# Sums of squares from token-major copies of x, modulation weights loaded ahead of x, and part of block 1's h made earlier

## The chip, the core and the metric

The kernel runs on one core of a Trainium2 chip. The core has a matrix engine (TensorE, PE in the profile), a vector engine (VectorE, DVE), a scalar engine (ScalarE, ACT), a general engine (GpSimd, POOL) and a queue that only issues transfers (SyncE, SP). Each takes its own instructions in order and waits on semaphores for the others; sixteen DMA engines move the data. The metric is the device time of one execution in microseconds (us), the median of the runs.

## The reference, cut to what matters

The layer takes 2048 tokens of 1024 features and 256 context tokens. For this document only its head matters, and that all of `h` enters one wide projection.

```python
def _rmsnorm(x, g):
    xf = x.astype(jnp.float32)
    xf = xf * lax.rsqrt(jnp.mean(xf * xf, axis=-1, keepdims=True) + EPS)
    return (xf * g.astype(jnp.float32)).astype(x.dtype)
...
mod = jax.nn.silu(c) @ w_ada[i] + b_ada[i]
mod_c = jax.nn.silu(c_ctx) @ w_ada[i] + b_ada[i]
shift, scale, gate = mod[:, None, :D], mod[:, None, D:2 * D], mod[:, None, 2 * D:]
h_lat = _rmsnorm(x, norm_g[i]) * (1.0 + scale) + shift
h_ctx = _rmsnorm(ctx, norm_g[i]) * (1.0 + scale_c) + shift_c
...
na_q, na_k, na_v, na_g, r_q, r_k, r_v, r_g = _split_proj(h_lat @ w_in)
```

So each token needs the mean square of its 1024 features, and each feature a scale and a shift, before its row of `h` can meet `w_in`. Attention, retention and the output projection follow.

## The kernel before

**Layout.** Matrix products want the features on the partitions, so the host gives a transposed copy `xT` beside `x`: nine groups of 256 tokens (0 to 7 latent, 8 the context), each of eight chunks k of 128 features. A group is held in two halves u of four chunks, 512 KB each. Two groups make a block of 512 tokens: block 0 is groups 0 and 1, block 1 groups 2 and 3, and so on; block 4 is the context.

**Precision.** Every wide product is made of three: a value is split into a high part (rounded to the fast matrix type, `hhi`, `whi`) and the rest (`hlo`, `wlo`), and high·high, high·low and low·high are added in PSUM. The high part is a copy on ACT, the low part a subtraction on DVE or POOL.

**What a group goes through.** `squares` (L194) squares it on ACT and adds the chunks on POOL (half 0) and DVE (half 1) until one 128 x 256 sum is left; `colsum` (L205) sums over partitions with four small matrix products; `rstd` (L212) takes the power -0.5 on DVE and POOL; `spread_copy` and `spread` (L218, L222) bring the result onto all partitions through PE. `spread_mul` (L238, L241) multiplies x by it; `prep_ab` (L267) applies scale and shift, some chunks on DVE (L272), the rest on ACT (L274); `prep_hl` (L276) makes the high part on ACT (L279) and the low part on DVE or POOL (L283, chosen by `LOV`), and notes a spill of the half to DRAM (`hS`, L253) at least eight steps later. The two groups of block 0 go chunk by chunk through `prep_first` (L255; L262 to L265) instead.

**Modulation.** Scale and shift come in four sets u of 256 features: four pieces of `w_ada` each (512 KB, `ada_load`), products on PE (`ada_mm`, L311, full fp32, or for the pieces named in `SPL` in split form after `ada_split`), a row copied out (`ada_row`, L319), turned by PE and finished on DVE (`ada_fin`, L324 to L332). Chunk k needs set k // 2.

**The windows.** `window(b)` (L491) is the first projection stage: for block b four units `u_k` (L380) of eight chunks k, three products (L363) per chunk, 32 steps per window; step n of window b is step 32b + n. Window 0 takes its units in the order `STEPS`, the others one unit after another. After a unit, ACT and DVE (L383, L384) split the result into a tile of `op` (two buffers) and SP stores it to `kS` (L151). The weight of units 0 and 1 is prepared in `w_split` (`wr[0]`), that of units 2 and 3 from `wr[1]`.

**The order.** `PLAN` (L39) lists every preparatory action with the step before whose successor it is put into the program (-1: before step 0); `run_acts` issues them. Names: sq squares, cs colsum, rs rstd and spread_copy, sp spread, mu spread_mul, ab and hl as above, s/m/ar/af the modulation, p prep_first, ws the weight split, x a load, blk a new block of h. Since each engine works in order, an action's place in the list is its place in every engine's queue. A step number is only a place in the program: an engine that is not waiting runs ahead of PE. SP carries the loads in `LOADS` order, then x loads, spills and kS stores as the program reaches them, and stops at the first whose data or buffer is not ready.

**Buffers.** Tiles named `st` (four buffers of 512 KB) take the raw weights, the squares of groups 2 to 7 and the context. Block 2 is written over the tiles in which x of groups 0 to 3 lay, so their spills must have landed first.

Of the kernel before, what the change touches and what calls it, by code (L numbers as in the profile page):

```python
# [18 lines left out]
P = 128  # L19
# [39 lines left out]
]  # L59
SPL = [9, 0, 1, 0]  # L60
ALO = [0, 5, 9, 4]
PFL = [3, 0, 0, 1, 0, 3, 1, 3]
STEPS = [0, 1, 2, 0, 1, 3, 2, 3, 2, 0, 3, 1, 1, 3, 0, 3, 2, 3, 0, 0, 2, 1, 1, 1, 1, 2, 3, 2, 2, 0, 3, 0]
WSL = [3, 2]
LEAD = 32
LOADS = [
# [16 lines left out]
def hybrid_kernel(ctx: ExitStack, tc: tile.TileContext, a: dict, out: bass.AP):  # L83
# [24 lines left out]
    sil4 = cst.tile([P, KC, 4], F32R, name="sil4")  # L108
    mods = cst.tile([P, 4, 3, 2, 2], F32, name="mods")
# [83 lines left out]

    def squares(i):  # L194
        sqs[i] = []
        for u in range(2):
            sq = xsq[i][u] if i < 2 else env["st"].tile([P, KH, 256], F32, name="st")
            nc.scalar.activation(sq, raw[i][u], AF.Square)
            eng = (nc.gpsimd, nc.vector)[u]
            eng.tensor_tensor(sq[:, 0:2, :], sq[:, 0:2, :], sq[:, 2:4, :], ALU.add)  # L200
            eng.tensor_tensor(sq[:, 0, :], sq[:, 0, :], sq[:, 1, :], ALU.add)
            sqs[i].append(sq)
        nc.vector.tensor_tensor(sqs[i][0][:, 0, :], sqs[i][0][:, 0, :], sqs[i][1][:, 0, :], ALU.add)

    def colsum(*ii):  # L205
        pm = ptile(None if ii[0] < 4 else psm)
        for j, i in enumerate(ii):
            for t in range(2):
                nc.tensor.matmul(pm[:, 2 * j + t:2 * j + t + 1], sqs[i][0][:, 0, t * P:(t + 1) * P], one, start=True, stop=True)
            rms[i] = pm[:, 2 * j:2 * j + 2]  # L210

    def rstd(i):  # L212
        r = env["st"].tile([P, 2], F32, name="rs", bufs=4)
        nc.vector.tensor_scalar(r, rms[i], 1.0 / D, EPS, ALU.mult, ALU.add)
        nc.gpsimd.tensor_tensor(r, r, mhalf[:, 0:2], ALU.pow)
        rbs[i] = r

    def spread_copy(i):  # L218
        rbs[i, 1] = env["st"].tile([P, 2, P], F32, name="t0", bufs=2)
        nc.vector.tensor_copy(rbs[i, 1], rbs[i].unsqueeze(2).to_broadcast([P, 2, P]))  # L220
# [34 lines left out]
    def prep_first(k):  # L255
        if k == KC - 1:
            spill.extend((i, u, now[0] + 8) for i in range(2) for u in range(2))
        for i in range(2):
            hi, lo = sub_dst(i)
            A, B = ab(i, k)  # L260
            x = raw[i][k // KH][:, k % KH, :]
            nc.scalar.activation(hi[:, k, :], x, AF.Identity, bias=B, scale=A)  # L262
            nc.vector.tensor_scalar(x, x, A, B, ALU.mult, ALU.add)
            eng = nc.gpsimd if PFL[k] >> i & 1 else nc.vector
            eng.tensor_tensor(lo[:, k, :], x, f(hi[:, k, :]), ALU.subtract)  # L265
# [27 lines left out]
    def ada_split(u, j):  # L293
        whl[u, j] = []
        for k in range(2):
            w = wad[4 * u + j][:, k, :]
            t = op.tile([P, 2, 512], F32R, name="o")
            nc.scalar.copy(t[:, 0, :], w)
            eng = nc.gpsimd if ALO[u] >> j & 1 else nc.vector
            eng.tensor_tensor(t[:, 1, :], w, f(t)[:, 0, :], ALU.subtract)  # L300
            whl[u, j].append(t)

    def ada_mm(u, j):
        if u not in aps:
            aps[u] = ptile(psm)
        for k in range(2):
            ops = [(silc, wad[4 * u + j][:, k, :])]
# [8 lines left out]
    def ada_row(u):  # L316
        rows[u] = op.tile([P, 2, 512], F32, name="o")[:, 0, :]
        n = 4 if SPL[u] else 2
        (nc.scalar.copy, nc.vector.tensor_copy)[u % 2](rows[u][0:n, :], aps[u][0:n, :])  # L319
# [132 lines left out]
    nc.sync.dma_start(silc, a["c2"])  # L452
    nc.scalar.activation(silc, silc, AF.Silu)
    nc.scalar.copy(sil4[:, :, 0:2], silc)
# [10 lines left out]
    for name, *args in LOADS:  # L465
        lds[name](*args)
    acts = dict(sq=squares, cs=lambda *i: colsum(*i), rs=lambda i: (rstd(i), spread_copy(i)), sp=lambda *i: spread(*i),
                mu=lambda i, u: spread_mul(i, (u,)), ab=prep_ab, hl=prep_hl, blk=alloc_blk, x=load_x, w=lambda: wr.append(w_raw(2560)),
                w2=lambda: load_w(), s=ada_split, m=ada_mm, ar=ada_row, af=ada_fin, p=prep_first,
                ws=lambda g: w01.append(w_split(wr[g], lo=WSL[g])))  # L470
    w01 = []
# [1152 lines left out]
```

## Time and profile before

| what | value |
|---|---|
| median of three runs | 1363.7 us (1363.22 to 1367.48) |
| the profiled execution | 1366.09 us |
| its span in the profile | 1364.1 us |
| mean granted TensorE clock | 0.993 |
| bytes moved by DMA | 287.25 MB, mean 211 GB/s |

The page of the profile gives busy shares over the whole span and the costliest groups of instructions. For a change at the head of the kernel the other views say more: the timeline of one engine (start, length, engine, line, operation, tiles, and in brackets how long the engine stood idle before it and what ended that), and the windows view (for each stretch of time the busy time of PE, weight loads, DVE, ACT and POOL with their instruction counts, then the granted clock of TensorE, the share of time in which the DMA engines were busy, and what they moved in GB/s). Transfers are shown where SP issues them, not where they land.

### The profile page before, as it was taken

To read this page: it belongs to the slowest core of one execution; us is meant where nothing else is said; L and a number is where in the kernel's file an instruction comes from. 1 tells how busy PE (TensorE), PEld (TensorE's weight loads), DVE (VectorE), ACT (ScalarE), POOL (GpSimd) and SP (SyncE) were. 2 spreads that over 40 slices of the span, in tenths; PEclk is the share of its full clock that TensorE was granted. 3 is DMA by queue.
4 is the path that set the end of the run, shared out by engine and by line. 5 is a ranking of instruction groups with operands and counts; after the bars stand their busy time and mean duration, and the time that the engine had idled before them with its cause. 6 is when DMAs were issued, how large, how long until landed. Compare 5 with 4: busy or idle time off the path is not lost.

```text
span 1364.1 us, 23087 instructions
## 1 busy us (share of the span) xinstructions
PE 1313.1 (96%) x8236; PEld 1148.9 (84%) x8236; DVE 827.9 (61%) x1442; ACT 606.5 (44%) x1259; POOL 583.8 (43%) x571
## 2 busy tenths in 40 slices
PE   6999999999999999999999999999999899999997
PEld 2477899887997788998999889889998789888886
DVE  5686356675766754377767777776644633445345
ACT  5354343243533344555655466556642234333332
POOL 5452102554034664355535465555422254544432
PEclk9999999999999999999999999999999999999999
DMA  9386788464867657967587778676538988455533
GB/s 364 132 277 232 260 296 222 165 208 151 326 179 228 217 197 230 273 198 194 157 225 208 210 202 245 171 215 188 140 110 277 267 264 286 159 170 170 162 121 128
DMA packets 197685, 287.25 MB, mean 211 GB/s; under 512 B 17345, under 2 KB 126017, under 8 KB 196290
## 3 DMA queue, kind: packets, MB, share of 16 engines
q1 hardware_dynamic: 165154, 228.35, 56.4%
q10 hardware_dynamic: 32416, 57.42, 11.7%
q8 instruction: 66, 1.08, 0.3%
q14 instruction: 49, 0.40, 0.1%
HBM read 194.48 MB, written 91.23 MB: 209 GB/s over the span
## 4 chain that ended last, share of the span: by engine, by line
PE 70%; DMA 9%; DVE 8%; ACT 4%; POOL 3%; issue 3%; SPq 2%; ACTq 0%; POOLq 0%; DVEq 0%
PE mm L374 17%; PE mm L671 13%; PE mm L1465 11%; PE mm L363 7%; PE sS L1025 4%; PE tr L1052 3%; PE po L1073 3%; PE mm L1188 2%; PE tr L1054 2%; PE po L1075 2%; DMA vB<-o 1%; PE mm L1377 1%; PE mm L1376 1%; PE mm L1375 1%; PE mm L311 1%
## 5 line engine op out<-in xcount | busy, mean ns | idle before, releaser
L374 PE MATMUL mm<-whi,hlo 128*128 128x256 f32 x832 | 228.5, 282 | 0.2 <-DMA hlo<-cS 0.2
L374 PE MATMUL mm<-whi,hhi 128*128 128x256 f32 x768 | 224.2, 292 | 0.0
L374 PE MATMUL mm<-wlo,hhi 128*128 128x256 f32 x768 | 216.9, 282 | 0.0
L1056 ACT CAST pt<-tr 128x640 fp32r<-128x640 f32 (+1 forms) x128 | 95.6, 747 | 160.9 <-PE tr L1054 158.4
L1062 DVE TENSOR_TENSOR pt<-tr,pt 128x640 fp32r<-128x640 f32 (+1 forms) x128 | 113.9, 890 | 78.5 <-ACT pt L1056 77.2
L374 PEld LDWEIGHTS mm<-whi,hlo 128*128 128x128 f32 x832 | 156.3, 190 | 0.6 <-DMA hlo<-cS 0.5
L1045 POOL TENSOR_SCALAR sp<-sp,stt 128x640 f32<-128x640 f32 (+2 forms) x128 | 103.2, 808 | 106.5 <-DVE stt L1044 74.5
L374 PEld LDWEIGHTS mm<-whi,hhi 128*128 128x128 f32 x768 | 146.2, 190 | 0.0
L374 PEld LDWEIGHTS mm<-wlo,hhi 128*128 128x128 f32 x768 | 145.9, 190 | 0.1
L1034 DVE CUSTOM_DVE_ANT_0 sp<-sS,nb 128x640 f32<-128x640 f32 (+2 forms) x128 | 105.6, 825 | 33.6 <-PE sS L1025 27.2
L1039 ACT ACTIVATE sp<-sp,stt 128x640 f32<-128x640 f32 (+2 forms) x128 | 107.4, 839 | 19.9 <-DVE stt L1034 18.7
L625 POOL TENSOR_TENSOR whi<-st,whi 128x512 fp32r<-128x512 f32 x48 | 63.9, 1353 | 107.3 <-ACT whi L624 107.3
L363 PE MATMUL mm<-hhi,whi 128*128 128x512 f32 x256 | 107.8, 421 | 0.0
L363 PE MATMUL mm<-hlo,whi 128*128 128x512 f32 x256 | 101.6, 397 | 6.0 <-DVE hlo L265 2.1
L1025 PE MATMUL sS<-k,q 128*128 128x256 f32 (+3 forms) x512 | 99.0, 315 | 5.3 <-DVE stt L1034 5.0
L363 PE MATMUL mm<-hhi,wlo 128*128 128x512 f32 x256 | 101.9, 398 | 0.3 <-DVE wlo L347 0.3
L671 PE MATMUL mm<-hhi,whi 128*128 128x512 f32 x336 | 98.4, 395 | 3.7 <-POOL whi L625 3.2
L1474 DVE TENSOR_TENSOR xt<-mm,xt 128x512 f32<-128x512 f32 x64 | 43.8, 686 | 87.4 <-PE mm L1465 87.3
L1465 PE MATMUL mm<-wor,y 128*128 128x512 f32 x384 | 95.6, 398 | 1.1 <-DVE xt L1474 1.1
L1025 PEld LDWEIGHTS sS<-k,q 128*128 128x128 f32 x512 | 82.7, 188 | 12.2 <-DVE stt L1034 8.4
L1465 PE MATMUL mm<-won,y 128*128 128x512 f32 x336 | 89.9, 406 | 0.0
L625 POOL TENSOR_TENSOR wlo<-st,wlo 128x512 fp32r<-128x512 f32 x36 | 53.6, 1488 | 77.4 <-ACT wlo L624 77.4
(258 smaller groups left out, 3057.5 us busy)
## 6 DMA issues: line engine op xcount, KB each, us to landing
st<-in_w_in_dram SPq DMA_DIRECT2D x64, 512.0 KB
q<-qS SPq DMA_DIRECT2D x64, 256.0 KB
hlo<-hS SPq DMA_DIRECT2D x20, 512.0 KB
k<-kS SPq DMA_DIRECT2D x16, 576.0 KB
kS<-o SPq DMA_DIRECT2D x16, 512.0 KB
vB<-o SPq DMA_DIRECT2D x64, 128.0 KB
qS<-o ACTq DMA_DIRECT2D x16, 512.0 KB
woS<-g ACTq DMA_DIRECT2D x32, 256.0 KB
```

Of the source, the lines that this page charges most:

```text
L363: nc.tensor.matmul(pm[:, :n], ww[:, k, cs], h[:, k, :], start=(k == 0 and i == 0), stop=(k == KC - 1 and i == 2))
L374: nc.tensor.matmul(pm[:, t * WG:(t + 1) * WG], h[:, k, o:o + P], ww[:, k, :], start=(k == 0 and i == 0), stop=(k == KC - 1 and i == 2))
L625: nc.gpsimd.tensor_tensor(t[:, 1], r, f(t)[:, 0], ALU.subtract)
L671: nc.tensor.matmul(pm, ww[:, k, :], hh[:, k, :], start=(k == 0 and i == 0), stop=(k == KH - 1 and i == 2))
L1025: nc.tensor.matmul(o, hd["q"][i][:, hl, j * P:(j + 1) * P], k, start=(hl == 0), stop=(hl == 1))
L1034: nc.vector.tensor_tensor_reduce(T["sp"][:, :n], T["s"], nbz[big][:, o:o + n], -1.0, 3e38, ALU.add, ALU.min, T["st"][:, 0:1])
L1039: nc.scalar.activation(sp[:, :n], sp[:, :n], AF.Exp, bias=st[:, 0:1], scale=-1.0, accum_out=st[:, 1:2])
L1045: nc.gpsimd.tensor_scalar(sp[:, :n], sp[:, :n], st[:, 2:3], 0.0, ALU.mult, ALU.add)
L1056: nc.scalar.copy(pt[:, :ng_ + 2, 0, :], tr[:, :ng_ + 2, :])
L1062: nc.vector.tensor_tensor(pt[:, :n, 1, :], tr[:, :n, :], f(pt)[:, :n, 0, :], ALU.subtract)
L1465: nc.tensor.matmul(pm, yy[:, k, :], ww[:, k, sl], start=(k == 0 and i == 0), stop=(k == 3 and i == 2))
L1474: nc.vector.tensor_tensor(xts[t][:, sl], pm, xts[t][:, sl], ALU.add)
```

## The change

For groups 2 to 8 a second load (`load_xt_`) brings the same 256 tokens from `x` itself, tokens on partitions, as two tiles of 128 x 1024 in `st`; ACT squares each with an accumulator, which gives the 128 sums at once. The adds and `colsum` of these groups go; `rstd` works in place. Groups 0 and 1 keep the old form, with both halves added on DVE and the spread copy on ACT.

The four pieces of modulation set 0 are loaded first, three of them ahead of group 1's x, and the pieces in split form change: before pieces 0 and 3 of set 0 and piece 0 of set 2, after it pieces 0 and 2 of set 3 (`SPL`). The others of set 3 use `silz`, a copy of `silc` with two columns of zeros, so that all of a set fill four rows.

The low parts move: `prep_first` takes group 1 first, with group 1's low part on POOL and group 0's on DVE; both halves of both weights in `ws` are subtracted on POOL, and are entered half by half; the split pieces are subtracted on DVE. `STEPS` becomes regular. In the plan, `ab` and `hl` of half 0 of groups 2 and 3 come at steps 14 to 17 (before: 24 to 28), the Squares of groups 2 and 3 at 9 and 10; from step 48 on the plan is as before except for the column sums that go and the `xt` loads at 60 and 81.

```diff
-SPL = [9, 0, 1, 0]
-ALO = [0, 5, 9, 4]
-PFL = [3, 0, 0, 1, 0, 3, 1, 3]
-STEPS = [0, 1, 2, 0, 1, 3, 2, 3, 2, 0, 3, 1, 1, 3, 0, 3, 2, 3, 0, 0, 2, 1, 1, 1, 1, 2, 3, 2, 2, 0, 3, 0]
-WSL = [3, 2]
+SPL = [0, 0, 0, 5]
+STEPS = [0, 1, 0, 1, 2, 3, 2, 3, 0, 1, 2, 3, 0, 1, 2, 3, 0, 1, 2, 3, 0, 1, 2, 3, 0, 0, 1, 1, 2, 2, 3, 3]
 LOADS = [
+    ('a', 0, 0), ('a', 0, 1), ('a', 0, 2), ('x', 1), ('c',), ('a', 0, 3), ('x', 0), ('a', 1, 0), ('a', 1, 1), ('w', 0), ('a', 1, 2),
+    ('a', 1, 3), ('w', 1), ('a', 2, 0), ('a', 2, 1), ('x', 2), ('a', 2, 2), ('a', 2, 3), ('x', 3), ('a', 3, 0), ('a', 3, 1), ('a', 3, 2), ('a', 3, 3),
 ]
+    (-1, 'm', 0, 0), (-1, 'm', 0, 1), (-1, 'm', 0, 2), (-1, 'sq', 1), (-1, 'm', 0, 3), (-1, 'cs', 1), (-1, 'rs', 1),
+    (-1, 'ar', 0), (-1, 'sq', 0), (-1, 'm', 1, 0), (-1, 'm', 1, 1), (-1, 'af', 0), (-1, 'sp', 1), (-1, 'cs', 0),
+    (-1, 'rs', 0), (-1, 'mu', 1, 0), (-1, 'ws', 0, 0), (-1, 'sp', 0), (-1, 'mu', 0, 0), (-1, 'p', 0), (-1, 'p', 1),
+    (-1, 'm', 1, 2), (-1, 'm', 1, 3), (0, 'ws', 0, 1), (0, 'ar', 1), (0, 'ws', 1, 0), (0, 'mu', 1, 1), (1, 'af', 1),
+    (1, 'p', 2), (2, 'mu', 0, 1), (3, 'p', 3), (3, 'ws', 1, 1), (3, 'xt', 2), (3, 'xt', 3), (3, 'x', 4),
+    (7, 'm', 2, 0), (7, 'm', 2, 1), (7, 'm', 2, 2), (7, 'm', 2, 3), (7, 'ar', 2), (8, 'af', 2), (8, 's', 3, 0),
+    (8, 'x', 5), (9, 'p', 4), (9, 'sq', 2), (10, 'sq', 3), (11, 'rs', 2), (11, 'm', 3, 0), (11, 'm', 3, 1),
+    (11, 'p', 5), (12, 'rs', 3), (12, 's', 3, 2), (13, 'sp', 2, 3), (13, 'mu', 2, 0), (13, 'xt', 4), (14, 'mu', 3, 0),
+    (14, 'ab', 2, 0), (15, 'm', 3, 2), (15, 'm', 3, 3), (15, 'blk', 1), (15, 'ab', 3, 0), (16, 'hl', 2, 0),
+    (16, 'ar', 3), (17, 'af', 3), (17, 'hl', 3, 0), (18, 'p', 6), (19, 'p', 7), (20, 'mu', 2, 1), (20, 'mu', 3, 1),
+    (20, 'sq', 4), (21, 'ab', 2, 1), (22, 'ab', 3, 1), (22, 'xt', 5), (23, 'hl', 2, 1), (24, 'hl', 3, 1),
+    (24, 'rs', 4), (28, 'x', 6), (32, 'sp', 4), (33, 'mu', 4, 0), (35, 'mu', 4, 1), (36, 'sq', 5), (40, 'ab', 4, 0),
+    (42, 'rs', 5), (46, 'xt', 6), (48, 'ab', 4, 1), (50, 'sp', 5), (52, 'mu', 5, 0), (52, 'sq', 6), (53, 'x', 7),
...
+    def load_xt_(i):
+        sqs[i] = []
+        src = a["ctx"] if i == 8 else a["x"][i * 256:(i + 1) * 256, :]
+        for t in range(2):
+            xt = env["st"].tile([P, KH, 256], F32, name="st").rearrange("p k t -> p (k t)")
+            nc.sync.dma_start(xt, src[t * P:(t + 1) * P, :])
+            sqs[i].append(xt)
+
     def squares(i):
+        if i >= 2:
+            rms[i] = env["st"].tile([P, 2], F32, name="rs", bufs=4)
+            for t, xt in enumerate(sqs[i]):
+                nc.scalar.activation(xt, xt, AF.Square, accum_out=rms[i][:, t:t + 1])
+            return
...
-            eng = (nc.gpsimd, nc.vector)[u]
+            eng = nc.vector if u or i < 2 else nc.gpsimd
...
-        nc.vector.tensor_copy(rbs[i, 1], rbs[i].unsqueeze(2).to_broadcast([P, 2, P]))
+        copy = nc.scalar.copy if i < 2 else nc.vector.tensor_copy
+        copy(rbs[i, 1], rbs[i].unsqueeze(2).to_broadcast([P, 2, P]))
...
-        for i in range(2):
+        for i in (1, 0):
...
-            eng = nc.gpsimd if PFL[k] >> i & 1 else nc.vector
+            eng = nc.gpsimd if i else nc.vector
...
+    def ws_half(g, u):
+        if u == 0:
+            w, wps[g] = w_parts(wr[g])
+            w01.append(w)
+        wps[g][u]()
```

More of the change, by code (lines that the diff above doesn't have):

```diff
@@ L108, in hybrid_kernel @@
     sil4 = cst.tile([P, KC, 4], F32R, name="sil4")
+    silz = cst.tile([P, KC, 4], F32, name="silz")
     mods = cst.tile([P, 4, 3, 2, 2], F32, name="mods")
@@ L205, in colsum @@
     def colsum(*ii):
-        pm = ptile(None if ii[0] < 4 else psm)
+        pm = ptile()
         for j, i in enumerate(ii):
@@ L212, in rstd @@
     def rstd(i):
-        r = env["st"].tile([P, 2], F32, name="rs", bufs=4)
+        r = rms[i] if i >= 2 else env["st"].tile([P, 2], F32, name="rs", bufs=4)
         nc.vector.tensor_scalar(r, rms[i], 1.0 / D, EPS, ALU.mult, ALU.add)
@@ L298, in ada_split @@
             nc.scalar.copy(t[:, 0, :], w)
-            eng = nc.gpsimd if ALO[u] >> j & 1 else nc.vector
-            eng.tensor_tensor(t[:, 1, :], w, f(t)[:, 0, :], ALU.subtract)
+            nc.vector.tensor_tensor(t[:, 1, :], w, f(t)[:, 0, :], ALU.subtract)
             whl[u, j].append(t)
@@ L306, in ada_mm @@
         for k in range(2):
-            ops = [(silc, wad[4 * u + j][:, k, :])]
+            ops = [(silz if SPL[u] else silc, wad[4 * u + j][:, k, :])]
             if SPL[u] >> j & 1:
@@ L318, in ada_row @@
         n = 4 if SPL[u] else 2
-        (nc.scalar.copy, nc.vector.tensor_copy)[u % 2](rows[u][0:n, :], aps[u][0:n, :])
+        (nc.scalar.copy if u else nc.vector.tensor_copy)(rows[u][0:n, :], aps[u][0:n, :])
     def ada_fin(u):
@@ L452, in hybrid_kernel @@
     nc.sync.dma_start(silc, a["c2"])
+    nc.vector.memset(silz, 0.0)
     nc.scalar.activation(silc, silc, AF.Silu)
+    nc.vector.tensor_copy(silz[:, :, 0:2], silc)
     nc.scalar.copy(sil4[:, :, 0:2], silc)
@@ L466, in hybrid_kernel @@
         lds[name](*args)
-    acts = dict(sq=squares, cs=lambda *i: colsum(*i), rs=lambda i: (rstd(i), spread_copy(i)), sp=lambda *i: spread(*i),
+    acts = dict(sq=squares, xt=load_xt_, cs=lambda *i: colsum(*i), rs=lambda i: (rstd(i), spread_copy(i)), sp=lambda *i: spread(*i),
                 mu=lambda i, u: spread_mul(i, (u,)), ab=prep_ab, hl=prep_hl, blk=alloc_blk, x=load_x, w=lambda: wr.append(w_raw(2560)),
                 w2=lambda: load_w(), s=ada_split, m=ada_mm, ar=ada_row, af=ada_fin, p=prep_first,
-                ws=lambda g: w01.append(w_split(wr[g], lo=WSL[g])))
-    w01 = []
+                ws=lambda g, u: ws_half(g, u))
+    w01, wps = [], {}
+    def ws_half(g, u):
[3 more added lines that the diff above has]
+        wps[g][u]()
     def run_acts(n):
```

2 lines of the change are left out of this document (1 added, 1 removed), and 29 rows, old and new, of tables (LOADS, PLAN).

## The prediction

> **What bounds the kernel now.** First the totals of the page.
>
> ```profile
> span 1364.1 us, 23087 instructions
> PE 1313.1 (96%) x8236; PEld 1148.9 (84%) x8236; DVE 827.9 (61%) x1442; ACT 606.5 (44%) x1259; POOL 583.8 (43%) x571
> ```
>
> TensorE is busy for 96% of the span, so an edit of other engines' work counts only where PE waits. The edit ends with step 127 of the plan, so I read the timeline of PE over the first 170 us for its waits.
>
> ```profile
> 27.44 0.49 PE L363 MATMUL mm<-hhi,whi 128*128 128x512 f32 x1
> 37.88 0.50 PE L363 MATMUL mm<-hlo,whi 128*128 128x512 f32 x1 [1.70 <-DVE hlo L265]
> 76.01 0.57 PE L363 MATMUL mm<-hlo,whi 128*128 128x512 f32 x1 [1.96 <-DVE hlo L283]
> 102.53 0.50 PE L363 MATMUL mm<-hlo,whi 128*128 128x512 f32 x1 [1.45 <-POOL hlo L283]
> 107.96 0.71 PE L227 MATMUL mm<-ident,t 128*128 128x128 f32 x4 [1.51 <-DVE t L220]
> 130.72 0.48 PE L363 MATMUL mm<-hhi,whi 128*128 128x512 f32 x1
> ```
>
> Products start at 27.44, a little before step 0 has all its h; window 1 (steps 32 to 63) waits for its h from 74.0 to 76.01, window 2 from 101.1 to 102.53, and 130.72 is the second step of window 3. Behind that PE runs without a gap to 170, so the change is worth what it moves the 130.72. Two waits cost more than their length, by the windows view:
>
> ```profile
> 35.19:38.60 3.41, 1.72 (x8) 0.63 (x6) 3.34 (x5) 1.53 (x3) 2.28 (x3) 1.00 1.03 411
> 38.60:42.01 3.41, 3.41 (x6) 0.36 (x5) 3.29 (x6) 0.00 (x0) 0.82 (x1) 0.51 1.03 412
> 76.14:79.55 3.41, 3.41 (x9) 2.62 (x10) 3.41 (x3) 2.41 (x4) 3.41 (x2) 0.51 0.99 243
> 100.03:103.44 3.41, 1.96 (x9) 1.30 (x9) 3.41 (x5) 0.27 (x2) 2.44 (x1) 1.00 0.16 66
> ```
>
> After a stretch of 3.41 us with PE half idle (1.72), the next ran at clock 0.51: 1.7 us lost. With 1.96 busy it did not.
>
> The second resource is the DMA queue of SP, which takes its entries strictly in order:
>
> ```profile
> 10.00:40.00 30.00, 27.31 (x89) 10.20 (x90) 21.94 (x37) 15.44 (x23) 18.39 (x14) 0.98 1.03 407
> 46.00:71.90 25.90, 25.52 (x109) 15.33 (x108) 18.89 (x39) 13.91 (x23) 10.90 (x13) 1.00 0.00 1
> 76.00:80.00 4.00, 3.99 (x11) 3.13 (x12) 4.00 (x3) 2.55 (x4) 4.00 (x2) 0.57 1.00 260
> 80.00:100.20 20.20, 20.20 (x96) 16.89 (x95) 15.91 (x25) 10.22 (x15) 7.62 (x7) 1.00 1.04 362
> ```
>
> ```profile
> 71.93 0.63 SPq L151 DMA_DIRECT2D kS<-o  x1
> 72.62 0.59 SPq L253 DMA_DIRECT2D hS<-hhi  x1
> 73.31 2.13 SPq L190 DMA_DIRECT2D chi<-in_xT_dram  x2
> ...
> 93.40 2.59 SPq L190 DMA_DIRECT2D clo<-in_xT_dram  x2
> ```
>
> From 46 to 71.9 nothing moves: SP stands at the first kS store, whose data are not there. From 71.93 on, 18 transfers of 512 KB (6 kS stores, 8 spills of h, two loads of x) fill the engines until 100.2. 0.524 MB at 362 GB/s is 1.45 us, and 2 + 18 x 1.45 = 28.1 us fits. This queue decides my forecast.
>
> **The change, part by part.**
>
> *Sums.* For groups 2 to 8 the adds and the column sums go.
>
> ```profile
> L200 POOL TENSOR_TENSOR st<-st 128x512 f32<-128x512 f32 x7 | 10.4, 1483 | 13.2 <-ACT st L198 13.2
> L209 PE MATMUL mm<-one,st 128*128 128x1 f32 x28 | 3.6, 238 | 0.4 <-DVE st L203 0.4
> L1421 ACT ACTIVATION_READ_ACCUMULATOR ot<-xt x32: 185/187/224, 1169.1 to 1358.3; 128x1 f32 x32
> ```
>
> PE saves 3.6 / 7, about 0.5 us a group, some 1 us of it behind 102.53 (groups 7 and 8). ACT keeps its two Squares a group, 1.0 each (the 90.55 row below), with 0 to 0.19 more each for the accumulator, which the trace has only on other shapes; I take 1.15. What is added is 1 MB of loads (xt) a group, two entries on SP's queue: 1.45 us apiece, with 1.29 (407 GB/s) and 2.02 (260 GB/s, the slowest stretch) as bounds.
>
> *The start.*
>
> ```profile
> 5.56 1.06 ACT L198 ACTIVATE hhi<-hhi 128x1024 f32<-128x1024 f32 x1 [2.62 <-DMA hhi<-in_xT_dram]
> 25.33 2.08 ACT L262 ACTIVATE hhi<-hhi,mods 128x256 fp32r<-128x256 f32 x4 [3.79 <-DVE hhi L241]
> ```
>
> The first load lands at 5.56, the next ones every 1.29 us. The eighth, the last of group 0's x, lands near 14.8, two entries later than now, because three weights stand ahead. ACT takes its Squares only behind the spread copy of group 1 (16.2, estimated), so adds, column sum, power, spread and the multiply end near 24.6, against 25.33 now; p0 then takes its 2 to 3 us: step 0 is complete between 27 and 28.3. I count no gain. The silz copies lie in DVE's idle first 5 us: nothing.
>
> *The weights' split.* Three split pairs become two, which costs PE 3.59 / 2 - 1.09 = 0.7 us; silz adds nothing to the width that PE streams.
>
> ```profile
> 34.87 1.09 PE L311 MATMUL mm<-o,sil 128*4 128x512 f32 x4
> 49.03 3.59 PE L311 MATMUL mm<-chi,silc 128*2 128x512 f32 x8
> 20.67 4.67 POOL L347 TENSOR_TENSOR wlo<-st,whi 128x1024 fp32r<-128x1024 f32 x2 [0.41 <-ACT whi L345]
> 46.59 0.57 ACT L319 COPY o<-mm 4x512 f32<-4x512 f32 x1 [9.87 <-PE mm L311]
> 29.20 0.62 ACT L298 CAST o<-hlo 128x512 fp32r<-128x512 f32 x1
> ```
>
> Four unsplit products of group 2 cost 4 x 1.77 = 7.1 us at step 7. Step 4 needs wlo of the second weight. POOL has all these subtractions now (2.33 each): the first till 26.1, low parts of p0 and p1 till 28.5, then two more till 33.2; PE comes at 31.5, a new wait of 1.7. So steps 4 to 7 end near 36 and group 2 near 43, with 8 of 32 steps done.
>
> *From there to the first kS store.* ACT stands at the row copy of group 2 until 43. Behind it, in order: the copy 0.6, a split 1.2, p4 1.0, the Squares of groups 2 and 3 2.3 each, p5 1.0: 51.4. Their xt are there: 28 loads ahead and four halves end near 46. DVE ends p5 at 52.4 and the power of group 3 follows (two small DVE operations beside POOL's 0.71, 1.5 with hand-overs): the spread at step 13 goes at 54, while PE arrived at 50.4: a new wait of 3.6, and by the half-idle rows a slow stretch.
>
> ```profile
> L241 DVE TENSOR_TENSOR hhi<-hhi,mm 128x1024 f32<-128x1024 f32 x8 | 9.6, 1209 | 0.5 <-PE mm L227 0.5
> L215 POOL TENSOR_TENSOR rs<-rs,mhalf 128x2 f32<-128x2 f32 x9 | 6.4, 707 | 25.1 <-DVE rs L214 25.1
> L263 DVE TENSOR_SCALAR hhi<-hhi,mods 128x256 f32<-128x256 f32 x16 | 8.8, 582 | 0.8 <-ACT hhi L262 0.7
> 71.20 2.41 POOL L283 TENSOR_TENSOR hlo<-hlo,hhi 128x1024 fp32r<-128x1024 f32 x1 [0.87 <-ACT hhi L279]
> 71.83 2.91 DVE L272 TENSOR_SCALAR hlo<-hlo,mods 128x256 f32<-128x256 f32 x4
> ```
>
> Then DVE: multiplies of groups 2 and 3 (2.4) and their scales to 59.5; the third row finish waits for PE's last products of group 3 and goes near 61.6; hl 1.2, p6 and p7 1.4 each (two scales of 0.58 at most, a subtraction), two multiplies 2.4, scales 1.5: 70. ACT's last cast of group 3 ends at 71.7, DVE's low part at 73; group 4's power waits for POOL behind its own 2.41; copy at 74.5, subtraction of unit 0 0.7: **kS store at 75.5**, against 71.93. The pair of rows above is a price in this: four scales took 2.91, 0.73 apiece, and the first could end only as POOL's subtraction did, at 73.6. Without such collisions I get 72, with one more 78. The gain is real meanwhile: h of block 1's first half is ready at 63.4 instead of 76.01, window 0 ends near 71.5 instead of 74.0. PE then waits at the spread of group 4 (step 32, to 75.3) and could begin window 2 near 97 to 98 instead of 101.1.
>
> *Window 2.* xt of group 6 is issued at step 46. Ahead of it in SP's queue from the first kS store: 5 kS stores, 7 spills (one has gone early) and x of group 6, 14 entries; it is the 15th and 16th. 75.5 + 2 + 16 x 1.45 = 100.7. ACT cannot pass its Square of group 6 (step 52), and behind it stand the casts that window 2 needs:
>
> ```profile
> 90.55 1.99 ACT L198 ACTIVATE st<-chi 128x1024 f32<-128x1024 f32 x2
> 93.32 1.98 ACT L279 CAST hhi<-hhi 128x1024 fp32r<-128x1024 f32 x2
> 98.08 1.05 ACT L279 CAST hhi<-hhi 128x1024 fp32r<-128x1024 f32 x1 [2.77 <-DVE hhi L272]
> 95.38 2.46 POOL L283 TENSOR_TENSOR hlo<-hhi 128x1024 fp32r<-128x1024 f32 x1 [1.25 <-ACT hhi L279]
> 99.20 3.27 POOL L283 TENSOR_TENSOR hlo<-hhi 128x1024 fp32r<-128x1024 f32 x1 [1.37 <-ACT hhi L279]
> ```
>
> Second Square to 101.9, ab 0.6, casts of 1.0 to 104.5 (group 4) and 105.5 (group 5), POOL 2.46 + 3.27 behind the first: h at **110**, against 102.53: +7.5. Behind it the waits at 107.96 (1.5) and for two column sums (1.0 with PE's own work) go: -2.5. PE has idled over 10 us: one stretch at half clock, +1.7. Sum at 130.72: **+6.7**. Nothing large behind takes it back, since PE is the bound there; I round it to +6.
>
> [...]
>
> **Rivals.** *The promised gain (faster).* If the spreads at steps 13 and 32 cost PE nothing, the first store goes at 67, at 1.29 us an entry xt lands at 89.6 and h at 99: -3.5 - 2.5 and up to 1.7 of clock: about -5, 1358.7. If no xt is late at all, the three old waits with their slow stretches go and window 2 starts up to 12 us sooner, 1352. For it: DMA idle from 46 to 71.9, and DVE and POOL relieved. Against it: 16 entries of which none can be passed, whatever engines do. It decides where xt lands before about 91.
>
> *No change.* The store at 72 as now, h at 106.5: +4 - 2.5, with the clock kept or lost 1.5 to 3.2: about 1366. For it: collisions of POOL and DVE may be fewer, as adds go.
>
> *Heavier.* The store at 78 or 79, or 2.02 us an entry for part of the queue: h at 114, +10, 1374. The context's xt comes five steps ahead of its Square (81, 86) behind spills too, and window 3's casts stand behind that Square: 2 us more.
>
> **How the numbers follow.** The profiled run took 1366.1 for a span of 1364.1; the median shown is 1363.7, and I add the difference to that. Forecast +6: **1369.7**, its own range 1367.8 to 1373, chance 0.36. Heavier 0.16, no change 0.28, faster 0.20. About 0.3% (4.1 us) is what a measurement here tells from no change: faster 0.20, same 0.28, slower 0.52. The range 1356 to 1377 leaves out the far ends of the first and last rival, some 0.1 each.
>
> **What would show it.** Right: the first kS store between 73 and 78; DMA near full from there to about 101; an idle ACT between steps 48 and 52 ended by the DMA of st; PE's longest wait ahead of window 2, on POOL or DVE hlo, ended between 106 and 113; smaller waits at step 4 on wlo and at the spreads of steps 13 and 32. Wrong: xt of group 6 landing before ACT comes to it, or the start more than 2 us off 27.44, or a first store before 70.

## The result and the profile after

| | before | after |
|---|---|---|
| median | 1364.5 us (1363.22 to 1367.48, four runs) | 1388.6 us (1380.56 to 1390.14, four runs) |
| ratio to before | | 1.0159, 95% interval 1.0136 to 1.0182 |
| the profiled execution | 1366.09 us | 1388.42 us |
| its span, mean clock | 1364.1 us, 0.993 | 1386.6 us, 0.984 |
| bytes moved by DMA | 287.25 MB | 294.57 MB |
| first product of window 1 starts | 73.66 us | 73.51 us |
| last product of window 4 starts | 163.86 us | 185.09 us |

The changed kernel is 1.6% slower, three to four times the loss that was forecast. Totals of the page, after:

```profile
span 1386.6 us, 23011 instructions
PE 1318.3 (95%) x8208; PEld 1153.7 (83%) x8208; DVE 811.3 (59%) x1422; ACT 607.1 (44%) x1274; POOL 559.6 (40%) x552
```

The last two rows of the table place the loss: window 0 is passed as before, and between the starts of window 1 and the end of window 4 lie 111.6 us instead of 90.2, which is 21.4 of the 22.5 us of span. The timeline of PE over the head of the changed kernel, its waits (L374 is the product of the windows, L363 before; L239 the spread):

```profile
33.70 0.50 PE L374 MATMUL mm<-hhi,wlo 128*128 128x512 f32 x1 [2.21 <-POOL wlo L358]
55.52 0.79 PE L239 MATMUL mm<-ident,t 128*128 128x128 f32 x2 [2.41 <-DVE t L232]
77.97 0.68 PE L239 MATMUL mm<-ident,t 128*128 128x128 f32 x4 [3.62 <-DVE t L232]
96.62 1.22 PE L239 MATMUL mm<-ident,t 128*128 128x128 f32 x4 [4.07 <-DVE t L232]
109.66 0.49 PE L374 MATMUL mm<-hhi,whi 128*128 128x512 f32 x1 [1.96 <-ACT hhi L291]
113.58 0.80 PE L374 MATMUL mm<-hlo,whi 128*128 128x512 f32 x1 [3.43 <-POOL hlo L295]
125.05 0.68 PE L239 MATMUL mm<-ident,t 128*128 128x128 f32 x4 [1.10 <-DVE t L232]
146.82 0.80 PE L374 MATMUL mm<-hhi,whi 128*128 128x512 f32 x1 [7.08 <-ACT hhi L291]
148.67 0.79 PE L374 MATMUL mm<-hlo,whi 128*128 128x512 f32 x1 [1.06 <-DVE hlo L295]
```

The four waits shown of before made 6.6 us in all (1.70, 1.96, 1.45, 1.51); these nine make 26.9: on the low weight at step 4, at the spreads of groups 2 and 3 (one wait), 4 and 5, before window 2 (5.4 us, and 1.45 in the kernel before), at the spread of group 7 (1.10) and before window 3 (8.1 us); at the last two places the kernel before had none. Who is late is read from the engine that PE waits for. ACT, its longest waits that a DMA ended, and the casts behind them (L204 is the Square, L394 the cast of a unit's result):

```profile
82.20 0.58 ACT L394 CAST o<-mm 128x512 fp32r<-128x512 f32 x1 [7.24 <-DMA kS<-o]
93.34 0.58 ACT L394 CAST o<-mm 128x512 fp32r<-128x512 f32 x1 [5.77 <-DMA kS<-o]
103.98 1.06 ACT L204 ACTIVATE st<-st 128x1024 f32<-128x1024 f32 x1 [6.42 <-DMA st<-in_x_dram]
106.69 2.92 ACT L291 CAST hhi<-hhi 128x1024 fp32r<-128x1024 f32 x3
141.30 1.06 ACT L204 ACTIVATE st<-st 128x1024 f32<-128x1024 f32 x1 [6.73 <-DMA st<-in_ctx_dram]
143.22 1.06 ACT L204 ACTIVATE st<-st 128x1024 f32<-128x1024 f32 x1 [0.78 <-DMA st<-in_ctx_dram]
145.74 1.98 ACT L291 CAST hhi<-clo 128x1024 fp32r<-128x1024 f32 x2
```

Before windows 2 and 3 ACT stands at a Square whose operand, the second load, has not landed; the casts that make the window's h stand behind it. The queue of SP shows why the loads were late:

```profile
78.46 0.63 SPq L149 DMA_DIRECT2D kS<-o  x1
...
96.25 1.14 SPq L197 DMA_DIRECT2D st<-in_x_dram  x2
...
126.09 1.47 SPq L174 DMA_DIRECT2D st<-in_ctxT_dram  x2
135.22 0.52 SPq L149 DMA_DIRECT2D kS<-o  x1
135.78 1.48 SPq L197 DMA_DIRECT2D st<-in_ctx_dram  x2
```

Group 6's two loads go at 96.25, behind 14 entries that begin with the kS store at 78.46. The context's two go at 135.78, and here nothing was in the way but one kS store, at which SP stands from 127.6. PE had finished its unit at 128.5, but ACT's cast of it went at 132.99 and DVE's subtraction at 134.51: ACT was late with all that it had queued, since the load of group 7 was late too (its Square at 120.62, after 5.00 us of idling), and since it stood another 2.21 us, to 129.96, for a spill of h that SP had issued behind group 7's two loads. So one late load delays ACT, ACT the cast of a unit, the cast the store, and the store the next load. This chain is read from one trace; no run below moves group 7's load alone.

Part of the loss is in no bracket. The windows view (PE's busy time, then the clock, the DMA share and GB/s):

```profile
31.56:34.97 3.41, 1.27 (x5) 1.00 1.02 419
34.97:38.38 3.41, 3.41 (x8) 0.50 1.03 418
52.04:55.45 3.41, 1.07 (x7) 1.00 0.92 339
75.94:79.35 3.41, 1.38 (x8) 1.00 0.02 5
93.00:96.41 3.41, 0.00 (x0) 1.00 1.07 390
106.66:110.07 3.41, 1.45 (x6) 1.00 0.12 50
110.07:113.49 3.42, 0.09 (x1) 0.50 0.00 0
113.49:116.90 3.41, 3.31 (x8) 0.50 0.33 122
```

Each of these stretches in which PE is busy for less than half of 3.41 us is followed by one at half clock (34.97, 110.07 and 113.49 are shown; by the trace's clock record also 55.45, 79.35 and 96.41). In all, 30.7 us before the end of window 4 are at half clock, and 6.8 us in the kernel before. A product of 128x512 starts there 0.43 us behind the one before it (76.38, 76.81 in the kernel before), and 0.23 us at full clock (73.43, 73.66).

### The profile page after: what moved, and what is told of

It reads as the page before. It is cut to its first block, busy times and chain, and to the rows that moved or that the text cites. A ratio compares the mean times of both kernels' runs of the same rounds, so it can differ in the third digit from the quotient of the medians.

```text
span 1386.6 us, 23011 instructions
## 1 busy us (share of the span) xinstructions
PE 1318.3 (95%) x8208; PEld 1153.7 (83%) x8208; DVE 811.3 (59%) x1422; ACT 607.1 (44%) x1274; POOL 559.6 (40%) x552
## 2 busy tenths in 40 slices
DMA packets 199699, 294.57 MB, mean 212 GB/s; under 512 B 17569, under 2 KB 126241, under 8 KB 198306
## 3 DMA queue, kind: packets, MB, share of 16 engines
q8 instruction: 65, 1.06, 0.3%
## 4 chain that ended last, share of the span: by engine, by line
PE 49%; DMA 7%; DVE 4%; POOL 3%; ACT 2%; issue 2%; SPq 1%; ACTq 0%; POOLq 0%; DVEq 0%
PE mm L385 11%; PE mm L1484 11%; PE mm L690 5%; PE sS L1044 4%; PE tr L1071 3%; PE mm L374 3%; PE po L1092 3%; PE mm L1207 2%; PE tr L1073 2%; PE po L1094 2%; DMA qS<-o 1%; DMA v<-rvS 1%; PE mm L1396 1%; PE mm L1395 1%; PE mm L1394 1%
## 5 line engine op out<-in xcount | busy, mean ns | idle before, releaser
L374 PE MATMUL mm<-hhi,whi 128*128 128x512 f32 x256 | 110.1, 430 | 9.0 <-ACT hhi L291 9.0
L374 PE MATMUL mm<-hlo,whi 128*128 128x512 f32 x256 | 104.8, 409 | 4.6 <-POOL hlo L295 3.4
L374 PE MATMUL mm<-hhi,wlo 128*128 128x512 f32 x256 | 104.1, 407 | 2.2 <-POOL wlo L358 2.2
L1484 PEld LDWEIGHTS mm<-wor,y 128*128 128x128 f32 x384 | 69.9, 188 | 18.1 <-issue 3.4
```

The source lines that it names most:

```text
L374: nc.tensor.matmul(pm[:, :n], ww[:, k, cs], h[:, k, :], start=(k == 0 and i == 0), stop=(k == KC - 1 and i == 2))
L1484: nc.tensor.matmul(pm, yy[:, k, :], ww[:, k, sl], start=(k == 0 and i == 0), stop=(k == 3 and i == 2))
```

## The experiments

Two theories at first. *Order*: the second loads stand late in SP's queue, and ACT stands at the Square; then an earlier place in the plan gives the loss back. *Rivals*: the 7.3 MB more that are loaded, or the new order of the engines, whatever the place of the loads. A third came from the windows view: the *clock* behind the waits. All results stand here. "Windows 1 to 4" is the time from the first product of window 1 to the last of window 4 in the profiled run, "half clock" how much of it was at half clock. The ratios decide on the time. The profile says where it went; outside of these windows it varies without order, the head up to window 1 by 3 us in kernels with the same head, and what follows window 4 from 1195.5 to 1205.4 us.

| kernel | median us | ratio to before (95%) | windows 1 to 4 | half clock |
|---|---|---|---|---|
| before | 1363.7 to 1365.1 | 1 | 90.2 | 3.4 |
| after | 1388.6 | 1.0159 (1.0136, 1.0182) | 111.6 | 23.9 |
| after, group 6 early | 1378.5 | 1.0119 (1.0085, 1.0153) | 103.2 | 20.5 |
| after, context early | 1381.0 | 1.0130 (1.0098, 1.0162) | 106.0 | 20.5 |
| after, all early | 1371.3 | 1.0060 (1.0035, 1.0085) | 96.0 | 10.2 |
| after, old sums | 1379.9 | 1.0125 (1.0093, 1.0157) | 90.0 | 3.4 |
| before, late loads | 1382.7 | 1.0135 (1.0115, 1.0155) | 106.9 | 20.5 |
| before, early loads | 1364.1 | 0.9998 (0.9978, 1.0018) | 90.8 | 6.8 |
| after, dummies | 1378.6 | 1.0111 (1.0092, 1.0131) | 108.7 | 6.8 |
| all early, power sooner | 1370.2 | 1.0045 (1.0029, 1.0061) | 96.5 | 13.7 |
| before, dummies | 1361.3 | 0.9969 (0.9956, 0.9983) | 88.1 | 0 |
| before, early, Square later | 1362.6 | 0.9980 (0.9965, 0.9995) | 86.5 | 3.4 |
| the same with dummies | 1359.6 | 0.9960 (0.9943, 0.9977) | 83.8 | 0 |
| all early, 5 of the 14 tiles left out | 1370.0 | 1.0037 (1.0016, 1.0057) | 92.7 | 6.8 |
| all early, dummies | 1366.5 | 1.0007 (0.9991, 1.0022) | 93.7 | 6.8 |
| the same, Square later | 1363.6 | 0.9987 (0.9972, 1.0002) | 91.6 | 3.4 |

### The place of the loads, in the new plan

```diff
-(24, 'rs', 4),  ...  (46, 'xt', 6)
+(24, 'rs', 4), (24, 'xt', 6),
```

> Changed kernel, only the second load of group 6 moved in the plan from step 46 to step 24, ahead of the spills and kS stores on SP. Order theory (the load is late because SP takes its queue in order and 14 entries stand ahead of it): it lands before 80, ACT no longer idles 6.4 us at the Square of group 6, window 2's first low part comes near 106 instead of 113.6, and the time is 7 to 9 us below the changed kernel, about 1380. Volume theory (7 MB more for the DMA engines, the place does not matter): the spills that it displaces become late by the same 2.8 us, and window 2 starts within 2 us of 113.6; about 1387. Plan theory (the new order on ACT, DVE and POOL is what costs; the first kS store is 6.5 us later): window 2 still starts after 111; above 1385.

Group 6 alone: PE begins window 2 without a wait, and the four windows are 8.4 us shorter. Window 3's wait stays (6.99 us at 136.45).

```diff
-(60, 'xt', 7), (61, 'hl', 5, 1),  ...  (81, 'xt', 8),
+(60, 'xt', 7), (60, 'xt', 8), (61, 'hl', 5, 1),
```

> Changed kernel, only the second load of the context (group 8) moved from step 81 to step 60, behind that of group 7 and ahead of the spills of groups 4 and 5 and four kS stores. Order theory: ACT's 6.7 us of idle time at the Square of group 8 goes, window 3 starts near 140 without its waits of 7.1 and 1.1 and without the three stretches at half clock from 144 to 154: 10 us below the changed kernel, about 1378. Volume theory: the spills of groups 4 and 5 land 2.8 us later, and the cast of group 6 that waits for them passes the delay on: at most 4 us better. Plan theory: no more than 3 us better.

The context alone: 5.6 us, though window 3's wait shrinks only to 3.58 us and does not go.

```diff
+(24, 'xt', 6),  ...  (40, 'xt', 7),  ...  (60, 'xt', 8),
```

> Changed kernel with the second loads of groups 6, 7 and 8 at steps 24, 40 and 60. Order theory: both gains add up, 16 to 18 us below the changed kernel, about 1371; what is left over the kernel before (7 us) are the waits of the head up to step 50. Volume theory: 1383 or more. Plan theory: 1383 or more, with ACT or DVE named at the starts of windows 2 and 3 and not a DMA.

All three: 15.6 us of the 21.4, and by the ratios 1.0 of 1.6%; singly the two edits gave 8.4 and 5.6 us (0.40 and 0.29%), so the sum holds within what the ratios can tell; this run also moves group 7's load, which no run moves alone. What is left in this run, ACT ahead of window 3:

```profile
123.35 1.05 ACT L291 CAST hhi<-chi 128x1024 fp32r<-128x1024 f32 x1 [6.14 <-DMA hS<-hhi]
...
127.86 1.05 ACT L204 ACTIVATE st<-st 128x1024 f32<-128x1024 f32 x1
...
131.40 1.03 ACT L291 CAST hhi<-clo 128x1024 fp32r<-128x1024 f32 x1
```

The loads no longer come late, but the cast waits 6.14 us for the spill of the tile that it overwrites (2.21 us in the changed kernel, 1.24 in the kernel before): in SP's queue the context's two loads (108.08) now stand ahead of these spills (109.61 to 115.0). And the two Squares of the context (now on time) still stand before window 3's casts.

### The loads alone, in the plan of before

Only groups 5 to 8 take the new sums; all else is the kernel before. Late, at the places that the change gave them:

```diff
-(42, 'cs', 5), (42, 'rs', 5),
+(42, 'rs', 5), (46, 'xt', 6),
...
+(22, 'xt', 5),  ...  (60, 'xt', 7),  ...  (81, 'xt', 8),
```

> Kernel before, its plan and modulation untouched; only groups 5 to 8 get the new sums, with their second loads at the steps that the change uses (22, 46, 60, 81). Order theory: the load of group 6 again stands behind 8 spills and 5 kS stores, lands near 98, and window 2 has its h near 108 instead of 102.5; the context's load lands near 126 and holds the start of window 3 by some 4 us; adds and column sums (2.5 us) are saved: 5 to 9 us above the kernel before, 1369 to 1373. Plan theory (the loads themselves cost little): the saved adds show, at or below the kernel before.

The direction was right, the size far too small: the late loads alone cost 1.35%, most of the whole loss. The waits of PE in that run are those of the changed kernel:

```profile
102.95 0.80 PE L376 MATMUL mm<-hhi,whi 128*128 128x512 f32 x1 [4.98 <-ACT hhi L292]
106.88 0.80 PE L376 MATMUL mm<-hlo,whi 128*128 128x512 f32 x1 [3.13 <-POOL hlo L296]
140.51 0.79 PE L376 MATMUL mm<-hhi,whi 128*128 128x512 f32 x1 [7.31 <-ACT hhi L292]
142.33 0.79 PE L376 MATMUL mm<-hlo,whi 128*128 128x512 f32 x1 [1.03 <-DVE hlo L296]
```

The same with the loads early, at 15, 24, 34 and 55:

> Kernel before with the new sums for groups 5 to 8, the second loads at steps 15, 24, 34 and 55, the first of them in the time from 46 to 72 us in which the DMA engines stand idle. Order theory: no Square waits for its load, and the waits of 1.45 at 102.5 and 1.5 at 108 and the column sums go: 1 to 4 us below the kernel before, 1360 to 1363. Volume theory: 2 us or more above the kernel before.

Level with the kernel before: the whole 1.35% hung on the place of eight loads. It wins nothing either, and ACT shows why:

```profile
116.56 1.05 ACT L292 CAST hhi<-chi 128x1024 fp32r<-128x1024 f32 x1 [3.17 <-DMA hS<-hhi]
...
121.06 1.05 ACT L206 ACTIVATE st<-st 128x1024 f32<-128x1024 f32 x1
122.10 1.05 ACT L206 ACTIVATE st<-st 128x1024 f32<-128x1024 f32 x1
...
124.60 1.98 ACT L292 CAST hhi<-clo 128x1024 fp32r<-128x1024 f32 x2
```

Window 2's low part starts at 99.10 instead of 102.53, and window 3 gives it back: it waits 2.35 and 1.02 us for casts behind the landing of a spill and two Squares.

### Volume

```diff
-(3, 'xt', 2), (3, 'xt', 3),  ...  and every later 'xt'
+(12, 'cs', 2, 3),  ...  (23, 'cs', 4),  ...  (42, 'cs', 5),  ...  (62, 'cs', 6),  (70, 'cs', 7),  (90, 'cs', 8),
```

> Changed kernel with the sums of groups 2 to 8 as before (squares of the transposed x, adds on POOL and DVE, column sums on PE) and no second loads; plan, STEPS, LOADS and modulation stay new. Order theory: windows 2 and 3 start without a wait for a load, but the adds (1.5 us of DVE a group) and column sums are back: 1369 to 1375, within 4 us of the kernel with all second loads early. Volume theory: at least 4 us faster than that kernel, since 7 MB are gone. Plan theory: still above 1383.

A miss. Without any second load, the new plan is still 1.25% slower, as PE now waits for the column sums:

```profile
51.34 0.61 PE L215 MATMUL mm<-one,st 128*128 128x1 f32 x4 [1.26 <-DVE st L209]
53.45 1.02 PE L215 MATMUL mm<-one,st 128*128 128x1 f32 x4 [1.50 <-DVE st L209]
73.94 1.01 PE L215 MATMUL mm<-one,st 128*128 128x1 f32 x4 [4.50 <-DVE st L209]
93.08 0.58 PE L215 MATMUL mm<-one,st 128*128 128x1 f32 x4 [2.14 <-DVE st L209]
```

Of the 14.1 us by which its span is longer, 9.2 lie ahead of window 1, which starts at 82.84 instead of 73.66, and 5.1 behind window 4, where the profiles vary without order; windows 1 to 4 take 90.0 us, as before. So the run took one cause away and brought another in: in the windows the new order loses nothing without the second loads, and ahead of them it needs the new sums. Whether the loads cost by place or by volume it can't tell. That question went to a cleaner edit:

```diff
         for t in range(2):
+            if t and i >= 4:
+                sqs[i].append(sqs[i][0])
+                continue
```

> The run with all three second loads early, but for groups 4 to 8 only the first of the two tiles is loaded a second time and its Square is taken twice, so that the sums of squares of the other 1024 columns are left out: half of the added bytes (3.7 MB less), the same work on ACT and the same order. If the 7 us that the early loads leave are the volume of the second loads, which delays spills and stores of kS, 3 to 4 us go: about 1367.5. If they lie in the new order of the engines, it stays at 1370 to 1372.

The edit does less than its expectation says. A tile holds 128 tokens with all their 1024 features, so the sums left out are those of the other 128 tokens of a group, and groups 4 to 8 lose five tiles: 2.6 MB by the profile (294.57 to 291.95), 36% of the added 7.3, not half. The ratio moves from 1.0060 to 1.0037, and the intervals overlap. The four windows are 3.3 us shorter in that profile (window 3's first product no longer waits, and 3.4 us less are at half clock), and by the medians 1.3 us come of it. If the whole 0.6% were volume, 36% of it would be 0.2%; if none were, nothing. This run can't tell the two apart. Against a large share of the volume stands a run of the next section, which moves all the bytes and is level with the kernel before.

### The clock

```diff
+FILLERS = {63: 24, 95: 28}
...
+            if now[0] in FILLERS:
+                pf = ptile()
+                for _ in range(FILLERS[now[0]]):
+                    nc.tensor.matmul(pf, w01[0][0][:, 0, 0:P], blk[b][0][:, 0, :], start=True, stop=True)
```

> Changed kernel with products whose result nobody reads put on PE where it waits: 24 behind step 63 and 28 behind step 95. Every other instruction and wait stays. If the clock is halved by a half-idle stretch, the stretches at half clock behind the starts of windows 2 and 3 (6.8 and 10.2 us in the trace) go, and with them what PE loses in them, 1.5 and 3.1: 3 to 5 us below the changed kernel, about 1384. If the waits alone cost the time: the same as the changed kernel or up to 2 us more.

The dummies stand where PE would have waited. They shorten none of ACT's waits (6.40 us for group 6's load and 6.97 for the context's, against 6.42 and 6.73), yet the ratio falls by 0.5%, some 6.5 us; the median fell by 10. The four windows are 2.9 us shorter, with 6.8 us at half clock instead of 23.9. Another 2.9 us of that profile are not the edit's: its window 1 began at 70.66 instead of 73.51, ahead of the first dummy (why, stands in the last section). The same edit on the kernel before, where 7, 9 and 5 dummies stand behind steps 7, 31 and 63:

> The kernel before with 21 dummy products of 128x512 that nobody reads: 7 behind step 7, 9 behind step 31, 5 behind step 63, where PE stands in the kernel before. The kernel before had 6.8 us of its head at half clock. If such a stretch costs about half its length, as the dummies of the changed kernel let it look, the time falls by 2 to 4 us, to about 1360.5. If the 10 us that the dummies brought in the changed kernel came from something else than the clock, the kernel before stays within 1 us of its time or is up to 3 us slower.

It is faster by 0.31% (interval 0.17 to 0.44%). Its profile has the four windows 2.1 us shorter: the first product of window 1 is no sooner (73.70), with the dummies ahead of it, but the second, for which PE waited in the kernel before, comes at 74.00 instead of 76.01. And on the changed plan with all loads early:

```diff
+FILLERS = {3: 6, 12: 7, 31: 9, 49: 11, 95: 6}
```

> The run with all three second loads early, with dummy products of 128x512 that nobody reads at the five places where PE stands in it: 6 behind step 3, 7 behind step 12, 9 behind step 31, 11 behind step 49, 6 behind step 95. That run had 24 us of its head at half clock against 6.8 us of the kernel before, and half of the difference, 8.5 us, is more than the 7 us that it is slower by. If the rest of the loss is the clock behind the new waits: 1361 to 1364, level with the kernel before or a little faster. If it is the new order and its waits themselves: 1368 to 1371.

From 1.0060 to 1.0007: of the 0.6% that the early loads left, the dummies took back 0.5, and the half clock up to the end of window 4 falls from 17.1 to 6.8 us (the 24 us of the expectation count 6.8 more behind it). This run moves all the second loads.

### What was left

```diff
-(24, 'rs', 4),  ...  (42, 'rs', 5),
+(20, 'rs', 4),  ...  (36, 'rs', 5),
```

> The kernel with all second loads early (1371.3), and the power and spread copy of groups 4 and 5 (rs) moved up in the plan, from step 24 to 20 and from 42 to 36, right behind their Squares, so that they no longer stand on DVE and POOL behind low parts, casts and kS stores. PE's waits at the spreads of groups 4 (3.6) and 5 (4.7) and the two slow stretches behind them go, and the first kS store comes 1 to 2 us sooner: 8 to 11 us below that kernel, 1361 to 1363, level with the kernel before or under it. If instead DMA paces windows 1 and 2 (op tiles freed by kS stores): under 3 us better.

A miss for the spreads: the wait at group 4's goes, that at group 5's falls from 4.67 to 2.05 us, and 0.15% comes of it, which the intervals don't tell from nothing. PE arrives sooner at window 2 and waits there:

```profile
100.57 0.49 PE L374 MATMUL mm<-hhi,whi 128*128 128x512 f32 x1 [0.94 <-ACT hhi L291]
104.59 0.80 PE L374 MATMUL mm<-hlo,whi 128*128 128x512 f32 x1 [3.52 <-POOL hlo L295]
```

ACT in that run still stands 6.47 and 4.63 us for landings of kS stores (80.89, 90.89). This fits the run's second expectation, that DMA paces the stretch; beyond these waits it isn't shown. Then the context's Square, which stood before window 3's casts, is moved behind them, in the plan of before with early loads:

```diff
-(55, 'xt', 8),  ...  (86, 'sq', 8),  ...  (92, 'rs', 8),  ...  (96, 'sp', 8),
+(69, 'xt', 8),  ...  (95, 'hl', 7, 1), (95, 'sq', 8), (97, 'rs', 8), (104, 'sp', 8),
```

> The order of before with the new sums and early second loads, but the context's two loads go behind the four spills of step 61's neighbourhood (entry at step 69) and its Square behind the last casts of window 3 (step 95 instead of 86), its row sums and spread at 97 and 104. Order theory: window 3 has its operands at 124 to 125.5 instead of 125.7 and 129.2, a gain of 3 to 4 us on the run with the same plan: about 1360. If the spills' landings set window 3 whatever stands ahead of its casts, it stays at 1363 to 1365.

Window 3's waits fall from 2.35 and 1.02 to 0.24 and 0.76 us. Its first product is no sooner than in the other run (125.53 against 125.69), its second step 1.9 us sooner (127.36 against 129.23). But PE also came 1.95 us later to window 3 in that profile (125.29 against 123.34), which alone takes as much off the first wait; the ratios, 0.9998 and 0.9980, have overlapping intervals. ACT's cast still waits 6.87 us for a spill (118.46), and the edit did not do all that its expectation says, as SP's queue shows:

```profile
107.94 2.61 SPq L199 DMA_DIRECT2D st<-in_ctx_dram  x2
110.60 0.48 SPq L266 DMA_DIRECT2D hS<-hhi  x1
```

Three of the four spills now go ahead of the context's loads, the fourth still behind them; by the trace's records it lands at 118.20, and the cast follows. So the Square's part is shown by the second step, and what the spill would do with no load ahead of it is not tested, here or in the next run, where the fourth spill stands behind the loads too. In the changed plan, with early loads and dummies:

> The run beside it with the context's two second loads at step 69 instead of 60 and its Square at 95 behind window 3's casts, row sums and spread at 97 and 104. If ACT's Square ahead of the casts is what holds window 3, 2 to 3 us less than the run beside it; if the spills' landings hold it, the same within 1 us.

From 1.0007 to 0.9987. Over the four windows the account, from one profile each, nearly closes: of 21.4 us, the place of the second loads 15.6 (111.6 to 96.0), the clock behind the short waits 2.3 (to 93.7), the Square ahead of the casts 2.1 (to 91.6, with 3.4 us less at half clock), which leaves 1.4. The first figure has clock in it too, 13.7 us less at half clock, which by half of its length is up to 6.8 us.

### A version faster than both

The plan of before, new sums for groups 5 to 8 loaded early, the context's Square behind window 3's casts, and 7 and 9 dummies behind steps 7 and 31:

> The kernel of the run beside it (context's Square behind window 3's casts) with 7 dummy products behind step 7 and 9 behind step 31. Both theories together, order and clock: 1356 to 1359, faster than the kernel before by 0.3 to 0.5%. If the dummies only fill and the clock is worth nothing, as the run beside it.

0.9960 of the kernel before (0.9943 to 0.9977), 5.6 us by the medians, and no half clock up to the end of window 4. PE's only waits at the starts of windows 2 and 3:

```profile
97.58 0.50 PE L377 MATMUL mm<-hlo,whi 128*128 128x512 f32 x1 [0.43 <-POOL hlo L297]
122.19 0.49 PE L377 MATMUL mm<-hhi,whi 128*128 128x512 f32 x1 [0.38 <-ACT hhi L293]
123.45 0.50 PE L377 MATMUL mm<-hlo,whi 128*128 128x512 f32 x1 [0.76 <-DVE hlo L297]
```

Most of the gain needs nothing of the change: the dummies alone gave 0.31%, the new sums with a good order 0.20%.

## Why the prediction was wrong

The sign was right, the size was not: 1369.7 was forecast, 1388.6 came, above the range's end of 1377.

- **The start** held: 27.07, no gain, and the wait at step 4 was 2.21 us against 1.7. The half-clock stretch behind it (34.97 to 38.38) was not charged.
- **The chain to the first kS store** held in kind. The spread at step 13 waited 2.41 us against 3.6, to 55.52 against 54; the store went at 78.46, where the text had 75.5 and, "with one more" collision, 78. Window 0 ended near 73.5 against 71.5.
- **The queue** held to the entry. 14 entries were ahead of group 6's loads, and the formula with the measured store, 78.46 + 2 + 16 x 1.45 = 103.7, is near what came: by the trace's records the two loads landed at 103.90 and 105.11, the first Square went at 103.98. From the second landing to the last operand of window 2 the text had 9.3 us and the trace 8.5 (113.58). So window 2 was 11.05 us late against +7.5, the place and size of the rival called heavier (h at 114, +10), and for its reason, a store at 78 to 79.
- **The step that failed** is the price of the context's load. In the heavier rival it is "2 us more", and in the forecast's sum it has no term. Behind the start of window 2 that sum has only -2.5 (waits that go) and +1.7 (clock), and "Nothing large behind takes it back" looks for a gain there, not for another loss. Between the first low product of window 2 and the second step of window 3 the loss grew from 11.05 (113.58 against 102.53) to 19.67 us (150.39 against 130.72): +8.6 us instead of -0.8, which is 9.4 of the 13.0 us between the +6.7 of the sum and the +19.7 measured; the other 3.6 are window 2's. PE's two waits for window 3's h, 7.08 and 1.06 us, are most of the 8.6. I had looked for spills ahead of that load; what held it was the kS store at 135.22, and what held that was ACT, late from group 7's load and from a spill behind it. Moving the context's load alone gave 0.29% back, all three 1.0%. I priced each late load by itself, where each one delays the next through the store between them.
- **The clock** was charged with 1.7 us for one more stretch; 23.9 us more at half clock came up to the end of window 4 (30.7 against 6.8). Dummies gave 0.5% back on the changed kernel and 0.5% again on the one with early loads. The half-busy rows were read rightly and applied to two waits out of nine. In the changed kernel 1.07, 1.27, 1.38 and 1.45 us of products in a stretch were followed by half clock, as 1.72 was in the kernel before.
- **The waits that go** went (the spread of group 6, 1.51 at 107.96, and the column sums), but a new one of 1.10 came at the spread of group 7. PE was to be at window 2 near 97 to 98; it stood at the spread of group 5 to 96.62, a wait that the text did not have, and came at 107.7. As far as the trace shows, this cost nothing by itself, since the h of window 2 was later still.

## What to carry over

When loads are added to a queue that issues in order, find for each one the entry ahead of it that waits for an engine, not only the bytes ahead of it: a load behind a store of results comes when that result is done, and if the engine that makes the result also stands at the loads, each late load makes the next one later (here ACT stood 6.42, 5.00 and 6.73 us at the Squares of groups 6 and 7 and of the context). Test the place of such a load before its volume; here the place was worth 1.0% in the new plan and 1.35% in the old one, and leaving out 36% of the bytes some 0.2%, which isn't certainly more than nothing. Count the waits that a new order makes, also short ones: in the heads of these kernels all 43 full-clock stretches of 3.41 us with 1.47 us or less of products were followed by half clock, up to 1.7 us more by half of its length, and products that nobody reads in the place of the waits took 0.31% off the kernel before and 0.5% off the changed one.

## What the runs showed of the hardware

Dummy products paid even in the kernel before: 21 products of 128x512, about 0.23 us each at full clock and so some 5 us of PE's time, made it 0.31% faster (interval 0.17 to 0.44%). They stand where waits were, and windows 1 to 4 have no half clock, where the kernel before has 3.4 us.

Whether a wait costs a slow stretch was partly luck in these runs. The head of the changed kernel and of the one with dummies is the same up to window 1, with the same waits (2.21 us at step 4, 2.41 at step 13). In the first they cost two slow stretches, in the second none, and that is the 2.9 us. The windows view of the second, on the boundaries of its own clock record:

```profile
31.72:35.13 3.41, 1.62 (x7) 1.00 1.03 423
35.13:38.55 3.42, 3.42 (x11) 1.00 1.03 417
52.20:55.61 3.41, 1.88 (x10) 1.00 0.66 270
55.61:59.03 3.42, 3.42 (x11) 1.00 0.07 25
```

In the clock record of the changed kernel every length up to 190 us is 3.41 us or a multiple of it. The edges fall otherwise in the two runs (34.97 against 35.13, while the wait at step 4 ends at 33.70 against 33.51), so this wait lies in one stretch (1.27 busy, above) or is split between two (2.99 busy from 28.31 on, and 1.62). A sharp limit isn't in these rows: 1.62 and 1.88 kept the clock here, and 1.72 lost it in the kernel before. Laid on the clock record of each of the fourteen kernels that have a slow stretch in their head, up to 190 us, the traces bound it for this case: all 43 full-clock stretches with 1.47 us or less of products were followed by half clock, between 1.52 and 1.90 it went either way, and none with more lost it. A stretch that was already at half clock was followed by another with up to 2.73 us of products in it, and by full clock from 2.83 on.

A subtraction on POOL and a scale on DVE did not run side by side here. In the changed kernel, ahead of window 2, the timeline of POOL:

```profile
108.74 4.79 POOL L295 TENSOR_TENSOR hlo<-hhi 128x1024 fp32r<-128x1024 f32 x2 [12.50 <-ACT hhi L291]
```

And that of DVE:

```profile
108.89 5.11 DVE L284 TENSOR_SCALAR hhi<-hhi,mods 128x256 f32<-128x256 f32 x3
```

Three scales, 0.41 us each where POOL stands still (one at 99.79), took 5.11 us: taken singly, the first two lasted 2.44 and 2.42 us, each to about the end of one of POOL's subtractions (2.44 and 2.39), and the third, with POOL done, 0.40. In the kernel before, the first of the four scales that start at 71.83 lasted 1.94 us, to 73.77, where POOL's subtraction ended at 73.61. What keeps them apart these rows don't show. The prediction had priced this collision for the first kS store, and it came back at window 2, where the last cast of group 5 waits for the scales (114.09).
